# The input projection of a hybrid attention and mLSTM step as products of scaled float16 pairs

## The chip, the cores and the metric

The kernel runs on one core of one Trainium2 chip. The metric is the time of one execution on the device in microseconds; the median of three runs stands for a kernel. A core has five engines with instruction streams of their own: TensorE (PE, its weight loads shown apart as PEld), VectorE (DVE), ScalarE (ACT), GpSimd (POOL) and SyncE (SP), which here starts nearly all the DMA transfers. Each engine takes its instructions in order.

## What is computed

One layer of a diffusion backbone is applied to 128 context tokens and 1024 latent tokens with a model width of 1024. All weights and activations are float32. The part that matters here is the input projection `h @ w_in` and what reads it:

```python
def trunk_layer(x, mods, norm1_w, w_in, ...):
    sh1, sc1, g1, sh2, sc2, g2 = mods
    h = rmsnorm(x, norm1_w) * (1 + sc1) + sh1
    aq, ak, av, mq, mk, mv, mo, mg = jnp.split(h @ w_in, SPLIT_POINTS, axis=-1)
    aq = rmsnorm(aq, q_norm_w)
    ak = rmsnorm(ak, k_norm_w)
    ...
    attn_o = attention(aq, keys, vals)
    gates = mg + gate_bias
    hm = mlstm_bidir(heads(mq), heads(mk) * (MLSTM_DK ** -0.5), heads(mv), gates, ...)
    hm = rmsnorm(hm, mlstm_norm_w) * sigmoid(mo)
    x = x + g1 * (concat([attn_o, hm]) @ w_out)
    h2 = rmsnorm(x, norm2_w) * (1 + sc2) + sh2
    return x + g2 * swiglu(h2, w_gu, w_down), ...
```

The modulation (`sh1`, `sc1` and so on) is `silu(cond) @ w_ada + b_ada`. `w_in` has 1024 rows and 2832 columns: 512 for the attention queries, 128 for keys, 128 for values, four times 512 for the four mLSTM heads (query, key, value, output gate, 128 columns of each to a head) and 16 for the gates.

## The kernel before

**Pairs.** TensorE multiplies in a reduced float32 form (`F32R`). To keep accuracy, each operand is split into a high part that the form holds exactly and a low part, the rest; a product is the sum of three: high by high, high by low and low by high. `load_piece` (L139) does this for weights. A DMA brings two blocks of 128 rows into `raw` (two buffers), ScalarE casts it to `whi` (L152), and the difference goes to `wlo` (L135, called from L154) on POOL, with every third one on VectorE; there are five buffers of each.

**Tokens.** The 1152 tokens are nine blocks of 128: block 0 is the context, 1 to 8 the latents. Three blocks make a chunk of 384 columns. The normalised and modulated `h` is kept transposed, as pairs of tiles `hTh` and `hTl` for each chunk (L291 and L292), in six buffers `b0` to `b5`; later tiles of the attention use these buffers again.

**Stages, in the order in which they are written.** First the rows of `w_ada` for the first two modulations are multiplied (L248) and turned into columns (L254), which `modulation` adds and scales into `scale1` and `shift1` (L240, L243). Then comes the stage of `h`, with the keys, values and gates: the loads of the four key/value pieces (L307 to L315, tiles `kraw`, the rows of x for blocks 1 and 2 between them), and for each block the norm (L257 to L264), the transposes on PE (L114), the modulation into `full` (three of eight columns blocks on ScalarE, L332, the others on VectorE, L335), the high half (L341 on ScalarE, L343 on VectorE) and the low half on POOL (L344). `linear_tok` (L389) multiplies blocks of tokens with pieces of weights (L399 to L401; the tokens are the stationary side, the weights stream), two blocks at a time, and hands the sums to an evacuation: `evac_kvg` copies keys and values (L408, L409) and adds the bias to the gates (L410).

Then the four mLSTM heads follow. `head_project` (L643) loads the head's four pieces of 2 by 512 columns (`head_pieces`), multiplies the queries transposed, chunk by chunk (`q_group`, L670 to L672, 384 columns), and then keys, values and output gates block by block (`linear_tok`, 384 columns), with the evacuation L649 to L663. The scan of head h (`head_mlstm`, L683) is woven between the products of head h+1. Head 3's scan stands beside the first part of the attention queries (`QFIRST`, 512 columns); the rest of the queries follow. After that come the attention, the output projection and the feed-forward part, in which `w_gu` and `w_down` are multiplied (L1189 to L1191, L1008 to L1010); the attention's probabilities are multiplied with the values there as float16 pairs already (L942, L943).

**What sets the order.** `weave` and `emit` write the generators' steps one between the other. A planner then simulates the program and orders each engine's instructions; `hot(n)` raises the priority of what is emitted under it. The pools reuse buffers by tag: a new tile of a tag waits for the last reader of the one whose buffer it takes.

Of the kernel before, what the change touches and what calls it, by code (L numbers as in the profile page):

```python
# [8 lines left out]
F32 = mybir.dt.float32  # L9
# [36 lines left out]
def hybrid_step(ctx: ExitStack, tc: tile.TileContext, I: dict, O: dict):  # L46
# [24 lines left out]
    def emit(gen):  # L71
        for _ in gen:
            pass
# [45 lines left out]
    def rsqrt(tp, ss, n, inv, cap=24, plus=EPS):  # L119
# [38 lines left out]


# [22 lines left out]
    selb = gp.tile([P, 36], BF16, name="selb")  # L182

# [107 lines left out]
    hTh = [hp.tile([P, KD, CT], F32R, name=f"hTh{c}", tag=f"b{2 * c}") for c in range(NCH)]  # L291
    hTl = [hp.tile([P, KD, CT], F32R, name=f"hTl{c}", tag=f"b{2 * c + 1}") for c in range(NCH)]  # L292
# [14 lines left out]
    kvg = []  # L307
    for j in range(4):
        rows = w_in[2 * j * P : (2 * j + 2) * P, :].rearrange("(a p) n -> p a n", p=P)
        kvg.append(load_piece([  # L310
            (lambda v: v[:, :, 0:256], rows[:, :, 512:768]),
            (lambda v: v[:, :, 256:272], rows[:, :, 2816:2832]),
        ], (2, 272), 2, p0.tile([P, 544], F32, name=f"kraw{j}")))
        if j % 2:
            dma(xs[j // 2 + 1], xrow(j // 2 + 1))  # L315

    for b in range(CB, NB):
        dma(xs[b], xrow(b))
    for c in range(NCH):
        if c > 0:  # L320
            normalise(c * CB, CB)
        for i in range(CB):
# [4 lines left out]
            for half, ps in enumerate(xT[b] if b < 1 else transposed(b)):  # L327
# [16 lines left out]
                sub(hTl[c][:, half * 4 : half * 4 + 4, i * P : (i + 1) * P], full, hi.bitcast(F32), "pool")  # L344
# [61 lines left out]
    def evac_kvg(b, ps):  # L406
        bi = 9 if b == 0 else b - 1
        nc.scalar.copy(kall[:, bi], ps[:, 0:128].rearrange("p (h d) -> p h d", d=HD))  # L408
        nc.scalar.copy(vall[:, bi], ps[:, 128:256].rearrange("p (h d) -> p h d", d=HD))  # L409
        dve.tensor_tensor(  # L410
            out=Gv[:, :, :, 4 * b : 4 * b + 4],
            in0=ps[:, 256:272].rearrange("p (d t h) -> p d t h", d=2, t=2),
            in1=gbias.rearrange("p (d t h) -> p d t h", d=2, t=2), op=ALU.add)

    emit(linear_tok(kvg, 0, 272, evac_kvg))


# [123 lines left out]
    def square_pieces(src):  # L541
        return [load_piece([(full_view, src[2 * j * P : (2 * j + 2) * P, :].rearrange("(a p) n -> p a n", p=P))], (2, 512))
                for j in range(4)]

    def norm_rope(qp, cc, ss, x, nb, nh, w, rb):
# [6 lines left out]
        ssum = qp.tile([P, 20], F32, name=nm("nrs"), tag="nrs", bufs=2)[:, :n]  # L552
# [22 lines left out]
    def k_work(qp, cc, ss, kw):  # L575
# [7 lines left out]
        qone = qp.tile([1, P], F32, name="qone")  # L583
        dve.memset(qone, 1.0)
# [16 lines left out]
        mm(ps[:, 0:2], qone, v1[:, 2:4], start=True, stop=True)  # L601
# [3 lines left out]
    def evac_q(qp, cc, ss, qw):  # L605
        held = {}

        def evac(b, ps):
# [4 lines left out]
            nc.scalar.copy(qr[:, b - grp[0]], ps.rearrange("p (h d) -> p h d", d=HD))  # L613
# [20 lines left out]
    def head_pieces(h):  # L634
        pieces = []
        for j in range(4):
            rows = w_in[2 * j * P : (2 * j + 2) * P, 768:2816].rearrange("(a p) (t g n) -> p a t g n", p=P, t=4, g=NH)
            pieces.append(load_piece(
                [((lambda v, a=a: v[:, a, :].rearrange("p (t n) -> p t n", t=4)), rows[:, a, :, h, :]) for a in range(2)],
                (2, 512)))  # L640
        return pieces

    def head_project(h, st):  # L643

        pieces = head_pieces(h)
# [3 lines left out]
        def evac(b, ps):  # L649
            kt = mlp.tile([P, P], F32, name=nm("kt"), tag="kt", bufs=MB)  # L650
            act(kt, ps[:, 0:P], AF.Copy, scale=P ** -0.5)
            va = mlp.tile([P, P + 1], F32, name=nm("va"), tag="va", bufs=MB)
            dve.tensor_copy(va[:, 0:P], ps[:, P : 2 * P])
            pool.memset(va[:, P : P + 1], 1.0)
            th = mlp.tile([P, P], F32, name=nm("th"), tag="th", bufs=2)
            act(th, ps[:, 2 * P : 3 * P], AF.Tanh, scale=0.5)
# [8 lines left out]
        def q_group(cs):  # L665
# [8 lines left out]
            for ps, c in zip(banks, cs):  # L674
                qT = mlp.tile([P, CT], F32, name=nm("qT"), tag="qTm", bufs=2 * NCH)
                dve.tensor_copy(qT, ps[:, 0:CT])
                st["q"][c] = qT
# [744 lines left out]
```

## Time and profile before

| | us |
|---|---|
| median of three runs (smallest, largest) | 1618.56 (1618.33, 1621.84) |
| the profiled execution | 1619.03 |
| its span, first to last instruction | 1617.1 |

The stages lie like this in the profiled execution:

| stage | us from the start of the span |
|---|---|
| products with `w_ada` for the first two modulations | 7 to 27 |
| `h`, keys, values, gates | 28 to 82 |
| mLSTM heads 0, 1, 2, 3, with the scan of the head before | 82 to 393 |
| attention queries | 393 to 466 |
| attention and output projection | 456 to 640 |
| feed-forward, with the rest of the attention | 622 to 1617 |

The profile's pages are read as follows. "Busy" is the time in which an engine had an instruction under way; matmuls overlap, so that the busy time of one is longer than the distance to the next. A group of instructions is named by its line in the code, engine and operation, by the tiles it writes and reads (`out<-in`), by its shape and its count; behind the bar stand the busy time and the mean length of one in ns, then the idle time before them with what ended it. In a timeline the first number is the start and the second the length. A table of windows gives, for each stretch of the span, the busy microseconds of each engine with its count of instructions, the mean clock granted to TensorE (1.00 is full), the busy share of the DMA engines and what they moved.

### The profile page before, as it was taken

Reading aid. Unit: us, or ns where it says so; the run is one execution under the profiler, and the core shown is the slowest. Engines: PE = TensorE matmul, PEld = TensorE weight load, DVE = VectorE, ACT = ScalarE, POOL = GpSimd, SP = SyncE. Lnnn points to the kernel's source line nnn. Section 1 sums busy time; section 2 is a strip of 40 time slices with the busy share of each in tenths; the row PEclk is TensorE's granted clock in tenths of the full one; section 3 lists DMA queues with packets and bytes.
Section 4 is the critical chain, followed back from the end, with each engine's and each line's share of the span. In section 5 each row is a group of like instructions: output and inputs, shape, how many; then the busy total and the mean of one; then the engine's idle time right before and its main releaser. Section 6 shows DMA issues by size and latency. Waiting matters only on the chain. (4 is left out here: it accounts for less than half of the span.)

```text
span 1617.1 us, 23358 instructions
## 1 busy us (share of the span) xinstructions
PE 1532.5 (95%) x8670; PEld 1366.1 (84%) x8670; DVE 965.3 (60%) x1969; ACT 689.8 (43%) x1193; POOL 618.0 (38%) x392
## 2 busy tenths in 40 slices
PE   6899999899898968999999999999999999999996
PEld 2888888898676757998989899898898989999995
DVE  4842363957877668577663646767674474432445
ACT  3522242424534556555643344565552453333322
POOL 1511030413345324443445344444344445544443
PEclk8999999999898988999999999999999999999998
DMA  9244443303155865777773446777684445534441
GB/s 358 67 155 125 117 142 52 82 22 71 50 183 134 180 153 116 174 181 178 180 179 113 148 153 216 188 179 175 156 185 131 131 144 176 151 127 146 144 130 65
DMA packets 386311, 232.71 MB, mean 144 GB/s; under 512 B 169910, under 2 KB 346502, under 8 KB 386198
## 3 DMA queue, kind: packets, MB, share of 16 engines
q1 hardware_dynamic: 384342, 228.04, 52.5%
q10 hardware_dynamic: 1856, 3.19, 0.6%
q8 instruction: 68, 1.11, 0.3%
q14 instruction: 45, 0.37, 0.1%
HBM read 181.16 MB, written 11.69 MB: 119 GB/s over the span
## 5 line engine op out<-in xcount | busy, mean ns | idle before, releaser
L135 POOL TENSOR_TENSOR wlo<-raw,whi 128x1024 fp32r<-128x1024 f32 (+1 forms) x159 | 390.2, 2459 | 512.3 <-ACT whi L152 474.4
L152 ACT CAST whi<-raw 128x1024 fp32r<-128x1024 f32 x239 | 245.0, 1026 | 361.7 <-DMA raw<-in_w_gu_dram 112.8
L1190 PE MATMUL mm<-aTl,whi 128*128 128x384 f32 (+2 forms) x1088 | 363.6, 334 | 0.0
L1189 PE MATMUL mm<-aTh,whi 128*128 128x384 f32 (+2 forms) x1088 | 362.5, 335 | 0.8 <-DVE tn L1217 0.8
L1191 PE MATMUL mm<-aTh,wlo 128*128 128x384 f32 (+2 forms) x1088 | 363.2, 334 | 0.0
L1189 PEld LDWEIGHTS mm<-aTh,whi 128*128 128x128 f32 x1088 | 204.5, 188 | 2.2 <-DVE tn L1217 1.4
L1190 PEld LDWEIGHTS mm<-aTl,whi 128*128 128x128 f32 x1088 | 204.9, 188 | 0.7
L1191 PEld LDWEIGHTS mm<-aTh,wlo 128*128 128x128 f32 x1088 | 204.9, 188 | 0.2
L135 DVE TENSOR_TENSOR wlo<-raw,whi 128x1024 fp32r<-128x1024 f32 (+1 forms) x80 | 98.4, 1230 | 151.7 <-ACT whi L152 147.8
L1008 PE MATMUL mm<-whi,hl 128*128 128x512 f32 x372 | 146.4, 398 | 0.8 <-ACT hl L1221 0.7
L1009 PE MATMUL mm<-wlo,hl 128*128 128x512 f32 x372 | 146.9, 396 | 0.0
L1010 PE MATMUL mm<-whi,hl 128*128 128x512 f32 x372 | 144.3, 396 | 0.8 <-POOL hl L135 0.8
L399 PE MATMUL wi<-whi,hTh 128*128 128x384 f32 (+2 forms) x392 | 135.9, 347 | 5.2 <-ACT hTh L341 5.1
L925 DVE SCALAR_TENSOR_TENSOR pl<-pr,st,ph 128x1152 f16<-128x1152 f32 (+1 forms) x72 | 111.6, 1550 | 47.7 <-ACT ph L924 47.6
L401 PE MATMUL wi<-whi,hTl 128*128 128x384 f32 (+2 forms) x392 | 133.6, 343 | 1.3 <-POOL hTl L135 1.3
L400 PE MATMUL wi<-wlo,hTh 128*128 128x384 f32 (+2 forms) x392 | 133.5, 341 | 0.0
L921 ACT ACTIVATE pr<-S,st 128x1152 f32<-128x1152 f32 (+1 forms) x72 | 81.2, 1128 | 99.7 <-DVE st L920 90.6
L135 POOL TENSOR_TENSOR hl<-tn,hl 128x384 fp32r<-128x384 f32 x66 | 83.5, 1266 | 105.0 <-ACT hl L1221 104.9
L998 DVE TENSOR_TENSOR x<-x,t 128x512 f32<-128x512 f32 x102 | 116.9, 1168 | 0.8
L1217 DVE SCALAR_TENSOR_TENSOR tn<-tn,mm 128x384 f32<-128x384 f32 (+2 forms) x68 | 36.6, 539 | 134.2 <-PE mm L1191 100.4
L918 PE MATMUL S<-kst,qT 128*128 128x384 f32 (+1 forms) x400 | 88.1, 356 | 13.9 <-ACT pr L921 13.8
L920 DVE TENSOR_REDUCE st<-S 128x1 f32<-128x1152 f32 (+1 forms) x72 | 88.8, 1233 | 20.7 <-PE S L918 20.3
(323 smaller groups left out, 2714.2 us busy)
## 6 DMA issues: line engine op xcount, KB each, us to landing
raw<-in_w_gu_dram SPq DMA_DIRECT2D x132, 512.0 KB, 4.0
raw<-in_w_down_dram SPq DMA_DIRECT2D x60, 512.0 KB, 3.6
a<-in_w_ada_dram SPq DMA_DIRECT2D x32, 512.0 KB, 4.2
gl<-g_d SPq DMA_DIRECT2D x36, 256.0 KB, 3.8
aw<-in_w_ada_dram SPq DMA_DIRECT2D x16, 512.0 KB, 8.9
raw<-in_w_in_dram SPq DMA_DIRECT2D x32, 256.0 KB, 5.6
raw<-in_w_out_dram SPq DMA_DIRECT2D x15, 512.0 KB, 4.9
x<-in_x_sample_dram SPq DMA_DIRECT2D x13, 512.0 KB, 6.4
```

Of the source, the lines that this page charges most:

```text
L135: (dve if eng == "dve" else pool).tensor_tensor(out=out, in0=full, in1=hi, op=ALU.subtract)
L152: nc.scalar.copy(hi[:, :n], raw[:, :n])
L399: mm(ps[:, :n], ah, wh[:, k % 2, c0 : c0 + n], start=(k == 0), stop=False)
L400: mm(ps[:, :n], ah, wl[:, k % 2, c0 : c0 + n], start=False, stop=False)
L401: mm(ps[:, :n], al, wh[:, k % 2, c0 : c0 + n], start=False, stop=(k == KD - 1))
L998: eng.tensor_tensor(out=x1[:, cs], in0=x1[:, cs], in1=t, op=ALU.add)
L1008: mm(ps, ah, wh[:, k % 2, :], start=(k == 0), stop=False)
L1009: mm(ps, ah, wl[:, k % 2, :], start=False, stop=False)
L1010: mm(ps, al, wh[:, k % 2, :], start=False, stop=(k == nk - 1))
L1189: mm(ps, wh[:, k, :], th[:, k, :], start=(k == 0), stop=False)
L1190: mm(ps, wh[:, k, :], tl[:, k, :], start=False, stop=False)
L1191: mm(ps, wl[:, k, :], th[:, k, :], start=False, stop=(k == KD - 1))
```

## The change

The products with `w_in` use pairs of float16 in place of pairs of reduced float32. Since float16 has a narrow range, both sides are scaled by powers of two first, and the evacuations take the scale out again.

- For `h`, the scale comes from a bound on the modulation: the greatest of `scale1` times the root of the width, plus the greatest of `shift1`. `powers` turns a bound into a power of two and its inverse with bit operations, and `scale1` and `shift1` are multiplied before the first `full`.
- For the weights, each group (key/value/gates, four heads, queries) gets one scale. `Scaled.ready` loads the four raw tiles, sums the absolute values of their rows on ScalarE, takes the maximum on VectorE and brings it to one number with `power_scale`: a transpose on PE, a maximum over the row, `powers`, and a product with a row of ones (`one1`) that spreads the two numbers over the partitions.
- `Scaled.pairs` makes the halves. Of every second piece, ScalarE makes the high half with the scale in the cast and VectorE the low half in one fused operation; of the others, ScalarE scales the raw tile in place and copies it, and POOL subtracts. For the key/value group all four go the first way.
- `hT` holds both halves in one float16 tile for each chunk, in buffers `b3` to `b5`.
- The key/value loads stand ahead of all the rows of x; the raw tiles of a head's weights are loaded and summed while the head before is multiplied; those of head 0 and the sums go beside the key/value products.
- Evacuations use scales from tiles. The gates' evacuation is two operations for each block instead of one. Two small buffers of `rsqrt` and the norm shrink from 24 and 20 columns to 16.

The number of products and their shapes stay: 1152 of 384 columns, 216 of 512 and 216 of 272. Each float16 matmul has its weight load as an instruction of its own.

```diff
+    def powers(v, n):
+        v = v[0:n]
+        dve.tensor_scalar(out=v[:, 0:1], in0=v[:, 0:1], scalar1=2.0 ** -16, scalar2=None, op0=ALU.max)
+        dve.tensor_scalar(out=v[:, 1:2].bitcast(I32), in0=v[:, 0:1].bitcast(I32), scalar1=0x7F800000, scalar2=None, op0=ALU.bitwise_and)
+        dve.tensor_scalar(out=v[:, 2:3].bitcast(I32), in0=v[:, 1:2].bitcast(I32), scalar1=-1, scalar2=266 * 2 ** 23, op0=ALU.mult, op1=ALU.add)
+        dve.tensor_scalar(out=v[:, 3:4], in0=v[:, 1:2], scalar1=2.0 ** -12, scalar2=None, op0=ALU.mult)
+
+    def power_scale(tp, one, bound, out):
+        ps = bank()
+        transpose(ps[0:1, 0:P], bound)
+        v = tp.tile([1, 4], F32, name=nm("pv"), tag="pv", bufs=2)
+        dve.tensor_reduce(out=v[:, 0:1], in_=ps[0:1, 0:P], axis=AX.X, op=ALU.max)
+        powers(v, 1)
+        yield
+        ps = bank()
+        mm(ps[:, 0:2], one, v[:, 2:4], start=True, stop=True)
+        dve.tensor_copy(out, ps[:, 0:2])
+        yield
+
+    class Scaled:
...
+        def ready(self):
+            a, b = self.shape
+            n = self.n = a * b
+            raws = self.raws or [wp.tile([P, 1024], F32, name=nm("iraw"), tag="wlo", bufs=5) for _ in self.srcs]
...
+                    dma(part(raw[:, :n].rearrange("p (a b) -> p a b", b=b)), ap_)
+            yield
+            t = gp.tile([P, 12], F32, name=nm("isc"), tag="isc", bufs=3)
+            for j, raw in enumerate(raws):
+                jk = wp.tile([P, 1024], BF16, name=nm("jk"), tag="raw", bufs=2)
+                act(jk[:, :n], raw[:, :n], AF.Abs, accum_out=t[:, j : j + 1])
+                yield
+            dve.tensor_reduce(out=t[:, 4:5], in_=t[:, 0:4], axis=AX.X, op=ALU.max)
+            dve.tensor_tensor(out=t[:, 4:5], in0=t[:, 4:5], in1=hsc[:, 3:4], op=ALU.mult)
+            yield from power_scale(gp, one1, t[:, 4:5], t[:, 6:8])
+            dve.tensor_tensor(out=t[:, 8:9], in0=t[:, 6:7], in1=hsc[:, 3:4], op=ALU.mult)
+            dve.tensor_scalar(out=t[:, 9:10], in0=t[:, 7:8], scalar1=P ** -0.5, scalar2=None, op0=ALU.mult)
+            dve.tensor_scalar(out=t[:, 10:11], in0=t[:, 7:8], scalar1=0.5, scalar2=None, op0=ALU.mult)
+            self.scale, self.inv, self.inv_k, self.inv_half = t[:, 8:9], t[:, 7:8], t[:, 9:10], t[:, 10:11]
+
+        def pairs(self, dve_every=2):
...
+                w = wp.tile([P, 2, 1024], F16, name=nm("ipair"), tag="whi", bufs=5)
+                hi, lo = w[:, 0, :n], w[:, 1, :n]
+                if j % dve_every == dve_every - 1:
+                    act(hi, raw[:, :n], AF.Copy, scale=self.scale)
+                    dve.scalar_tensor_tensor(out=lo, in0=raw[:, :n], scalar=self.scale, in1=hi, op0=ALU.mult, op1=ALU.subtract)
+                else:
+                    act(raw[:, :n], raw[:, :n], AF.Copy, scale=self.scale)
+                    nc.scalar.copy(hi, raw[:, :n])
+                    sub(lo, raw[:, :n], hi, "pool")
...
-    hTh = [hp.tile([P, KD, CT], F32R, name=f"hTh{c}", tag=f"b{2 * c}") for c in range(NCH)]
-    hTl = [hp.tile([P, KD, CT], F32R, name=f"hTl{c}", tag=f"b{2 * c + 1}") for c in range(NCH)]
+    hT = [hp.tile([P, 2, KD, CT], F16, name=f"hT{c}", tag=f"b{3 + c}") for c in range(NCH)]
+    hTh, hTl = [t[:, 0] for t in hT], [t[:, 1] for t in hT]
+
+    dve.tensor_reduce(out=hs2, in_=shift1, axis=AX.XY, op=ALU.max, apply_absolute_value=True)
+    dve.tensor_reduce(out=hsc[:, 0:1], in_=scale1, axis=AX.XY, op=ALU.max, apply_absolute_value=True)
+    dve.scalar_tensor_tensor(out=hsc[:, 0:1], in0=hsc[:, 0:1], scalar=float(D) ** 0.5, in1=hs2, op0=ALU.mult, op1=ALU.add)
+    powers(hsc, P)
+    for t in (scale1, shift1):
+        dve.tensor_scalar(out=t, in0=t, scalar1=hsc[:, 2:3], scalar2=None, op0=ALU.mult)
...
+    kvg_steps = kvg.ready()
+    next(kvg_steps)
+    for b in range(1, CB):
+        dma(xs[b], xrow(b))
     for b in range(CB, NB):
         dma(xs[b], xrow(b))
...
+    steps = groups_in[0].ready()
+    next(steps)
...
+            if b == 0:
+                with hot(300):
+                    emit(kvg_steps)
+                    kvg_pairs = kvg.pairs(1)
...
-        nc.scalar.copy(kall[:, bi], ps[:, 0:128].rearrange("p (h d) -> p h d", d=HD))
+        act(kall[:, bi], ps[:, 0:128].rearrange("p (h d) -> p h d", d=HD), AF.Copy, scale=kvg.inv)
...
-    emit(linear_tok(kvg, 0, 272, evac_kvg))
+    weave(linear_tok(kvg_pairs, 0, 272, evac_kvg), steps, 40, 8)
+    emit(steps)
...
     def head_project(h, st):
-        pieces = head_pieces(h)
+        w = groups_in[h]
+        pieces = w.pairs()
+        nxt_steps = groups_in[h + 1].ready()
+        next(nxt_steps)
...
-            act(kt, ps[:, 0:P], AF.Copy, scale=P ** -0.5)
+            act(kt, ps[:, 0:P], AF.Copy, scale=w.inv_k)
-            dve.tensor_copy(va[:, 0:P], ps[:, P : 2 * P])
+            dve.tensor_scalar(out=va[:, 0:P], in0=ps[:, P : 2 * P], scalar1=w.inv, scalar2=None, op0=ALU.mult)
...
-        yield from linear_tok(pieces, P, 3 * P, evac)
+        for i, _ in enumerate(linear_tok(pieces, P, 3 * P, evac)):
+            if i % 4 == 3:
+                next(nxt_steps, None)
+            yield
+        emit(nxt_steps)
```

More of the change, by code (lines that the diff above doesn't have):

```diff
@@ L182, in hybrid_step @@
     selb = gp.tile([P, 36], BF16, name="selb")
+    one1 = gp.tile([1, P], F32, name="one1")
+    hsc = gp.tile([P, 4], F32, name="hsc")
+    hs2 = gp.tile([P, 1], F32, name="hs2")
+    dve.memset(one1, 1.0)
     es0 = ExitStack()
@@ L600, in k_work @@
         ps = bank()
-        mm(ps[:, 0:2], qone, v1[:, 2:4], start=True, stop=True)
+        mm(ps[:, 0:2], one1, v1[:, 2:4], start=True, stop=True)
         dve.tensor_copy(vsc[:, 0:2], ps[:, 0:2])
```

66 lines of the change are left out of this document (32 added, 34 removed).

## The prediction

> **What bounds the kernel now.** I read the page first, then a table of windows of 10 us, then single engines' timelines at the seams it showed.
>
> ```profile
> span 1617.1 us, 23358 instructions
> PE 1532.5 (95%) x8670; PEld 1366.1 (84%) x8670; DVE 965.3 (60%) x1969; ACT 689.8 (43%) x1193; POOL 618.0 (38%) x392
> ```
>
> The profiled execution took 1619.03 us, so 1.9 us lie around its span, and it stands 0.5 us above the median of 1618.56. TensorE is nearly always busy, but an average of 95% says nothing of a stage. The windows do (columns: PE, PEld, DVE, ACT, POOL, granted clock, DMA share, GB/s):
>
> ```profile
> 30.00:40.00 10.00, 4.61 (x18) 3.97 (x18) 8.96 (x34) 8.75 (x17) 4.32 (x3) 0.55 1.01 377
> 50.00:60.00 10.00, 8.38 (x59) 7.72 (x57) 9.79 (x23) 2.75 (x7) 5.83 (x4) 0.92 0.35 96
> 70.00:80.00 10.00, 10.00 (x83) 10.00 (x81) 7.16 (x20) 5.76 (x13) 6.76 (x7) 1.00 0.10 31
> 300.00:310.00 10.00, 8.05 (x52) 7.27 (x50) 9.93 (x31) 5.63 (x13) 4.86 (x6) 1.00 0.37 107
> 420.00:430.00 10.00, 7.18 (x52) 5.96 (x52) 9.88 (x49) 7.57 (x29) 3.02 (x6) 1.00 0.08 29
> ```
>
> Three regimes follow. From 30 to about 70 us the h and key/value stage hangs on VectorE (9.79 of 10). From 70 us through three heads PE is full at clock 1.00: there a shorter matmul is worth its full length. Around 290 to 330 and 390 to 430 us VectorE is full again (9.93, 9.88) and PE has holes: there a shorter matmul is worth nothing and an added VectorE operation costs its length. Behind 640 us PE is full with products that the change doesn't touch, so a delay or gain ahead of them arrives at the end undiminished.
>
> **The narrower products.** A busy matmul row overlaps the next, so I take the distance from start to start (columns: start, us, then the instruction). The first pair of rows lies 15 matmuls of 384 columns apart, the second 15 of 512, the third 27 fp32r of 256, the last 8 float16 of 256:
>
> ```profile
> 100.48 0.33 PE L399 MATMUL wi<-whi,hTh 128*128 128x384 f32 x1
> 103.08 0.34 PE L399 MATMUL wi<-whi,hTh 128*128 128x384 f32 x1
> 445.14 0.39 PE L400 MATMUL mm<-wlo,hTh 128*128 128x512 f32 x1
> 448.64 0.40 PE L400 MATMUL mm<-wlo,hTh 128*128 128x512 f32 x1
> 630.27 0.28 PE L1189 MATMUL mm<-aTh,whi 128*128 128x256 f32 x1
> 633.46 0.28 PE L1189 MATMUL mm<-aTh,whi 128*128 128x256 f32 x1
> 1169.81 0.27 PE L942 MATMUL po<-phT,vs 128*128 128x256 f16 x1
> 1170.69 0.27 PE L942 MATMUL po<-phT,vs 128*128 128x256 f16 x1
> ```
>
> That is 2.60/15 = 173 ns, 3.50/15 = 233 ns, 3.19/27 = 118 ns and 0.88/8 = 110 ns. So float16 gains 8 ns on 118. The trace has no float16 matmul of 384 or 512 columns. If the gain is a fixed 8 ns, 384 columns come to 165 ns; if it goes with width (0.932 times), to 161 ns and 217 ns. I take a saving of 10.5 ns at 384 and 14.5 ns at 512, between both ends (8 to 12, 8 to 16), nearer the proportional one because the fp32r rows themselves lie on a line of 0.45 ns a column. The Trainium skill ("TensorE: Matmul & The Clock Gate", section "Back-to-back issue gap") gives N/2.4 + 2.5 ns for a warm isolated matmul, 109 ns at 256, which the 110 ns agree with; by it 384 and 512 columns would take an estimated 162.5 and 216 ns.
>
> How many there are (columns: count, then busy us and mean ns):
>
> ```profile
> L399 PE MATMUL wi<-whi,hTh 128*128 128x384 f32 x288 | 100.6, 349 | 0.0
> L670 PE MATMUL wi<-hTh,whi 128*128 128x384 f32 x96 | 33.8, 353 | 0.0
> L399 PE MATMUL mm<-whi,hTh 128*128 128x512 f32 x40 | 17.3, 433 | 4.0 <-DVE nu L758 2.5 <-ACT qraw L613 1.5
> L399 PE MATMUL wi<-whi,hTh 128*128 128x512 f32 x32 | 12.7, 398 | 0.0
> ```
>
> Each line is one of three products, so the four heads have 3 x (288 + 96) = 1152 matmuls and the queries 3 x 72 = 216. A head saves 288 x 10.5 ns = 3.0 us. Heads 0 and 1 run wholly in full-PE time; of the 6.0 us of heads 2 and 3 I count 4.6, since each meets a stretch in which VectorE rules. Heads: **-10.6 us**. Of the queries only the 3 x 40 of the second pass run with PE as the bound: **-1.7 us**. The 216 key/value matmuls of 272 columns shorten inside the VectorE-bound stage: 0. With nothing but this, 1619.0 would become 1606.7.
>
> **The start of the h stage.** Now the first modulated `full` on VectorE stands early:
>
> ```profile
> 30.61 0.41 DVE L335 TENSOR_SCALAR full<-mm,scale,shift 128x128 f32<-128x128 f32 x1
> 31.21 0.15 DVE L126 TENSOR_SCALAR rh<-rv 128x1 int32<-128x1 int32 x1
> 31.39 0.15 DVE L127 TENSOR_SCALAR ry<-rh 128x1 int32<-128x1 int32 x1
> 32.06 0.64 ACT L152 CAST whi<-kraw 128x544 fp32r<-128x544 f32 x1 [0.55 <-DMA kraw<-in_w_in_dram]
> 32.97 0.63 ACT L152 CAST whi<-kraw 128x544 fp32r<-128x544 f32 x1
> ```
>
> In the changed order VectorE reaches `full` only behind the maximum over the four absolute row sums of the key/value pieces and then ten small dependent operations (the maxima of scale1 and shift1, the power of two, two multiplications). The fourth piece is in by 32.97 now; it moves ahead of x1 in SyncE's queue, so I let its Abs end near 32.6. Small dependent operations start 0.18 to 0.19 us apart (31.21, 31.39). That gives 32.6 + 10 x 0.19 = 34.5 for the first `full`: +3.9 us. Lower end +2, if the pieces land as much sooner as two x loads of 512 KB take; upper end +6, if the sums wait behind x's Square on ScalarE. Queued behind are the transposes' evacuations, the float16 halves, and PE's key/value products.
>
> To the end of the stage VectorE gets: four fused lo halves (L217) in place of two subtractions, some 20 small operations of two scale chains, and two operations per G evacuation where there was one.
>
> ```profile
> 75.16 1.20 DVE L343 CAST hTh<-full 128x512 fp32r<-128x512 f32 x1 [0.53 <-ACT full L332]
> 76.44 1.29 POOL L135 TENSOR_TENSOR hTl<-full,hTh 128x512 fp32r<-128x512 f32 x1 [0.36 <-DVE G L410]
> 34.06 0.71 DVE L135 TENSOR_TENSOR wlo<-kraw,whi 128x544 fp32r<-128x544 f32 x1
> L410 DVE TENSOR_TENSOR G<-wi,gbias 128x16 f32<-128x16 f32 x9 | 1.4, 164 | 0.0
> ```
>
> Two more halves at 0.71 are 1.4 us, nine small operations for the stage's own chain and seven for head 0's 16 x 0.17 = 2.7, nine more G operations 1.5: 5.6 in all. VectorE has 0.2 to 1.3 us of air per 10 us here, and POOL loses two subtractions that ran beside it, so I count +3. The last lo half on POOL then lies near 84.6.
>
> Head 0 follows. ScalarE used to make a hi half with one cast; now it makes, in this order, a scaled copy in place of pieces 0 and 2 and then the hi half of piece 0, and POOL's lo half follows.
>
> ```profile
> L152 ACT CAST whi<-raw 128x1024 fp32r<-128x1024 f32 x227 | 237.6, 1048 | 334.0 <-DMA raw<-in_w_gu_dram 112.8 <-PE mm L1190 56.1 <-DMA raw<-in_w_down_dram 49.3
> L135 POOL TENSOR_TENSOR wlo<-raw,whi 128x1024 fp32r<-128x1024 f32 x153 | 382.6, 2504 | 500.6 <-ACT whi L152 462.7 <-issue 14.7 <-DVE t L997 12.9
> L135 DVE TENSOR_TENSOR wlo<-raw,whi 128x1024 fp32r<-128x1024 f32 x74 | 94.3, 1274 | 127.1 <-ACT whi L152 123.3 <-DMA a<-in_w_ada_dram 3.5
> 81.83 0.34 PE L670 MATMUL wi<-hTh,whi 128*128 128x384 f32 x1
> ```
>
> 3 x 1.05 + 2.50 = 5.6 us against 1.05 + 1.27 = 2.3 now, 3.3 us more, about half of it under the last key/value products: +1.7. So the first product of head 0 moves from 81.8 to about 90.4. Start in all: **+8.6 us**, ends +5 and +11.
>
> **The heads.** Each group costs ScalarE four Abs with a sum, which the Square of x prices, and two more passes; and evacuations take their scale from a tile instead of a constant.
>
> ```profile
> L261 ACT ACTIVATE jk<-x 128x1024 bf16<-128x1024 f32 x9 | 9.5, 1056 | 1.4 <-DMA x<-in_x_sample_dram 0.9 <-DMA x<-in_x_prompt_dram 0.2
> L261 ACT ACTIVATION_READ_ACCUMULATOR jk<-x 128x1 f32 x9 | 1.7, 190 | 0.0
> L651 ACT ACTIVATE kt<-wi 128x128 f32<-128x128 f32 x36 | 9.4, 277 | 74.9 <-PE wi L401 74.9
> L751 ACT ACTIVATE it<-mm,QT 128x129 f32<-128x129 f32 x64 | 20.1, 369 | 7.4 <-PE mm L748 5.7 <-DVE nu L758 1.2 <-DVE dn L765 0.3
> L653 DVE COPY va<-wi 128x128 f32<-128x128 f32 x36 | 10.1, 283 | 16.9 <-ACT kt L651 13.9 <-PE mm L755 2.8
> L335 DVE TENSOR_SCALAR full<-mm,scale,shift 128x128 f32<-128x128 f32 x45 | 16.2, 402 | 1.9 <-ACT full L332 1.6
> L925 DVE SCALAR_TENSOR_TENSOR pl<-pr,st,ph 128x1152 f16<-128x1152 f32 x64 | 105.3, 1645 | 47.1 <-ACT ph L924 47.0
> ```
>
> ScalarE: 4 x (1.06 + 0.19) + 2 x 1.05 = +7.1 us a group, and 18 evacuations at up to 369 in place of 277, +1.7. It was 43% busy and the raws of the next head are loaded, summed and scaled during the current one, so PE's own work hides it; without that cover it would be 9 us a head. VectorE: eleven small operations (1.9), two fused halves at 1.32 (1645 x 1024/1152, 1.46, at most) for 1.33 subtractions at 1.27 (+1.2), nine va copies at up to 402 for 283 (+1.1): +4.2 a group, free where PE is full. In the two stretches of VectorE it is not: the part that falls there (one chain, nine evacuations, one of the two halves, and the query group's) I put at +1.8 and +1.5, **+3.3 us** (ends 0 and +6). The four products with `one1` and the transposes before them sit in PE's order and wait for VectorE's small operations; a late one holds up every matmul behind it. I count half a microsecond for each of four or five, **+2.2** (ends 0 and +8). POOL has 2 instead of 2.67 subtractions a group: nothing, as it isn't the bound.
>
> From 456 us on only buffers change (three tiles of h leave), and the order of PE's products stays: 0, ends -4 and +4.
>
> **Sum:** 1619.0 - 10.6 - 1.7 + 8.6 + 3.3 + 2.2 = 1620.8; I say **1621 us**.
>
> **Rivals.**
> *A, the delays hide.* If the raws' earlier loads and the spare time on POOL let the stage end only 4 us late, and VectorE's additions find the holes, the toll is 4 + 1 and the time 1619.0 - 12.3 + 5 = 1612. For it: PE was full already at 70 us, ahead of the last h halves. Against: VectorE at 9.79, in order.
> *B, the scaled pairs come late at every head.* The pair tiles have five buffers for four pieces, so a head's first pairs wait for the last products of the head before; then the copy, the float16 half and POOL's 2.5 us run with PE idle. If each of four boundaries shows 3 us of hole more, that is 12 us: 1633. It decides once ScalarE reaches the next pieces less than 3.6 us (1.05 + 2.50) before PE has run out. For it: ScalarE's 9 us more a head, and its evacuations in the same queue. Against: PE shows no hole at any boundary of the first three heads now.
> *C, float16 at 384 columns is no faster than fp32r,* because each product now carries a weight load as an instruction of its own, of this length (columns: count, busy us, mean ns):
>
> ```profile
> L942 PEld LDWEIGHTS <-vs 128*128 128x128 f16 x292 | 29.1, 100 | 26.0 <-issue 9.5 <-DVE oT L947 6.1 <-DMA phT<-ph 5.9
> ```
>
> Then the 12.3 us are gone: 1633. Against: the 110 ns rows carry such loads too.
> *D, float16 products of 384 columns overlap until only the 100 ns of the weight load part them.* That saves 73 ns on each of 1152, and from 1633 the heads alone lead to 1549. Against: at 256 columns they stand 110 ns apart, not 100, and a row of 233 ns at 512 shows no such overlap. The same section of the Trainium skill states a sustained 131 ns per matmul at 512 columns for pairs of load and matmul, which would go this way; no row here bears it out.
>
> **How the numbers follow.** Forecast 0.45, its own range 1614 to 1628; A 0.26; B 0.18; C 0.09; D 0.02. Within 0.2%, 3.2 us, is what a measurement can't tell from no change (1615.3 to 1621.8). Of the forecast's own case I put 0.04 below, 0.19 within and 0.22 above; A gives 0.25 faster and 0.01 within, B and C are slower, D faster: 0.31, 0.20, 0.49. The range runs from 1608 (A with proportional savings and a start of +3) to 1635 (B with the upper end of the stretches); about 0.15 is left out.
>
> **What would show it.** First `full` near 34.5 us, first product of head 0 near 90, start distances of 161 to 165 ns at 384 and about 218 at 512, PE full to about 290, and the two VectorE stretches longer by 1 to 2 us each. A start under 86 speaks for A; holes of 3 us at head boundaries for B; 173 ns for C. The prediction is wrong if the attention stage from 456 us moves by more than 4 us either way, since I gave it nothing.

## The result and the profile after

| | before | after |
|---|---|---|
| median, us (smallest to largest of 5 runs) | 1618.56 (1618.16 to 1623.24) | 1627.82 (1622.25 to 1632.99) |
| span of the profiled execution, us | 1617.1 | 1626.0 |

The ratio is 1.0046, with a 95% interval of 1.0028 to 1.0065: slower by half a per cent. It lies inside the range, 0.2 us below the end of the forecast's own (1614 to 1628), and on the side that had the greatest chance, but by another sum than the one that was forecast. Measured again beside three other kernels, the same kernel came to 1622.43 us, 1.0010 times the kernel before (1.0000 to 1.0020). So the loss is 0.1 to 0.5%, and the executions of the changed kernel seem to scatter more: over 10.7 us in 5 runs and 8.5 in 11, where those of the kernel before kept within 5.1 in 5 and within 6.8 to 8.9 in three rounds of 23.

The head of the page and the table of windows of the changed kernel (window, then PE, PEld, DVE, ACT, POOL, granted clock, DMA share, GB/s):

```profile
span 1626.0 us, 23528 instructions
PE 1517.4 (93%) x8688; PEld 1258.8 (77%) x8688; DVE 970.8 (60%) x2059; ACT 732.5 (45%) x1251; POOL 606.5 (37%) x387
```

```profile
30.00:40.00 10.00, 1.33 (x4) 0.68 (x4) 7.56 (x47) 8.75 (x19) 2.27 (x2) 0.58 1.01 385
50.00:60.00 10.00, 7.81 (x58) 5.82 (x58) 9.69 (x30) 6.61 (x15) 3.46 (x3) 0.95 0.17 48
70.00:80.00 10.00, 10.00 (x88) 8.45 (x86) 8.22 (x33) 6.45 (x16) 6.72 (x8) 1.00 0.09 24
300.00:310.00 10.00, 4.15 (x17) 2.28 (x18) 9.61 (x18) 7.36 (x16) 4.83 (x3) 0.73 0.33 84
```

TensorE is busy 15 us less in a span that is 9 us longer. The window from 30 us shows the late start, that from 70 us that the start was made up, and that from 300 us holds the seam before head 3, which lay later and was spread wider before; the part on the prediction compares the whole of it.

Following a few instructions of TensorE through both traces shows where the time went. The table gives their starts in us. The last query product stands for the last of the high-by-high ones; two more follow within half a microsecond. The 112th score product is the last of the first attention chunk, and behind the 161st TensorE is nearly full to the end (the recorded expectations count that one as the 160th):

| | before | after | difference |
|---|---|---|---|
| first key/value product | 34.2 | 39.4 | +5.2 |
| first product of head 0 | 81.8 | 82.4 | +0.6 |
| first token product of head 3 | 327.7 | 321.2 | -6.5 |
| last query product | 465.4 | 455.7 | -9.7 |
| 112th score product | 601.1 | 599.4 | -1.7 |
| 161st score product | 700.3 | 705.9 | +5.6 |
| end of the span | 1617.1 | 1626.0 | +8.9 |

The change does what it was meant to up to the last query product, 9.7 us ahead. Then the attention stage gives back 15.3 us, and the feed-forward part another 3.3. These 3.3 us are within the scatter: in the fourteen profiles here that part takes 916.8 to 921.1 us, the least in the kernel before. The windows from the last query product to the 161st score product, the first of the kernel before, the second of the changed one, in fences of their own:

```profile
465.00:700.00 235.00, 203.63 (x1122) 171.53 (x1120) 169.78 (x300) 124.75 (x185) 97.43 (x54) 0.92 0.69 163
```

```profile
456.00:706.00 250.00, 207.53 (x1125) 173.61 (x1124) 164.24 (x306) 126.27 (x189) 97.65 (x55) 0.90 0.63 148
```

The number of products is about the same (1122 and 1125). Of the 15 us more, TensorE idles 11.1 (42.5 against 31.4), and for the rest it is "busy" at a lower clock. What it waits for there, grouped by waiter and releaser (us in total, times, longest), in the kernel before and then in the changed one:

```profile
PE S L918 <- ACT pr L921: 12.2, 7, 2.9
PE po L942 <- DMA phT<-ph: 4.9, 2, 4.5
PE po L942 <- DVE oT L947: 4.8, 2, 4.3
```

```profile
PE S L1000 <- ACT pr L1003: 17.7, 8, 3.7
PE po L1025 <- DMA plT<-pl: 6.2, 5, 2.2
PE po L1024 <- DMA phT<-ph: 5.9, 3, 5.2
PE po L1024 <- ACT pr L1003: 4.5, 1, 4.5
```

These are links of the softmax chain: scores wait until ScalarE has taken the exponentials of the last ones, the values wait for the transposed probabilities. The change touches none of these instructions. The experiments ask why they cost more.

### The profile page after: what moved, and what is told of

Read it like the earlier page. It is cut to its first block, busy times and chain, and to the rows that moved or that the text cites. A ratio compares the mean times of both kernels' runs of the same rounds, so it can differ in the third digit from the quotient of the medians.

```text
span 1626.0 us, 23528 instructions
## 1 busy us (share of the span) xinstructions
PE 1517.4 (93%) x8688; PEld 1258.8 (77%) x8688; DVE 970.8 (60%) x2059; ACT 732.5 (45%) x1251; POOL 606.5 (37%) x387
## 5 line engine op out<-in xcount | busy, mean ns | idle before, releaser
L135 POOL TENSOR_TENSOR wlo<-raw,whi 128x1024 fp32r<-128x1024 f32 x146 | 357.8, 2454 | 445.7 <-ACT whi L152 407.9
L152 ACT CAST whi<-raw 128x1024 fp32r<-128x1024 f32 x219 | 224.4, 1025 | 375.9 <-DMA raw<-in_w_gu_dram 137.8
L135 DVE TENSOR_TENSOR wlo<-raw,whi 128x1024 fp32r<-128x1024 f32 (+1 forms) x73 | 88.1, 1206 | 142.2 <-ACT whi L152 141.7
L1007 DVE SCALAR_TENSOR_TENSOR pl<-pr,st,ph 128x1152 f16<-128x1152 f32 (+1 forms) x72 | 107.8, 1498 | 39.4 <-ACT ph L1006 39.4
L488 PE MATMUL wi<-ipair,hT 128*128 128x384 f16 (+2 forms) x392 | 128.2, 327 | 2.8 <-ACT ipair L216 2.8
L489 PE MATMUL wi<-ipair,hT 128*128 128x384 f16 (+2 forms) x392 | 128.1, 327 | 0.0
L490 PE MATMUL wi<-ipair,hT 128*128 128x384 f16 (+2 forms) x392 | 127.1, 326 | 0.0
L135 POOL TENSOR_TENSOR hl<-tn,hl 128x384 fp32r<-128x384 f32 x66 | 84.2, 1276 | 105.0 <-ACT hl L1303 105.0
```

The lines of the kernel that those rows point to most:

```text
L135: (dve if eng == "dve" else pool).tensor_tensor(out=out, in0=full, in1=hi, op=ALU.subtract)
L152: nc.scalar.copy(hi[:, :n], raw[:, :n])
L488: mm(ps[:, :n], ah, wh[:, k % 2, c0 : c0 + n], start=(k == 0), stop=False)
L489: mm(ps[:, :n], ah, wl[:, k % 2, c0 : c0 + n], start=False, stop=False)
L490: mm(ps[:, :n], al, wh[:, k % 2, c0 : c0 + n], start=False, stop=(k == KD - 1))
```

## The experiments

For each kernel below, the table gives the start of the last query product, the length from there to the 161st score product ("stage"), and the span, all from its profile, with the median and the ratio of its runs to the kernel before on the same chip.

| kernel | last query product | stage | span | median | ratio (95%) |
|---|---|---|---|---|---|
| before | 465.4 | 234.9 | 1617.1 | 1618.56 | 1 |
| changed | 455.7 | 250.2 | 1626.0 | 1627.82 | 1.0046 (1.0028 to 1.0065) |
| a_again, the same | 452.9 | 246.3 | 1617.3 | 1622.43 | 1.0010 (1.0000 to 1.0020) |
| a_const | 445.8 | 253.5 | 1620.4 | 1621.34 | 1.0004 (0.9991 to 1.0017) |
| a_tags | 457.6 | 245.0 | 1622.8 | 1620.20 | 1.0000 (0.9987 to 1.0013) |
| a_tags_const | 446.7 | 247.7 | 1613.8 | 1614.69 | 0.9969 (0.9955 to 0.9983) |
| a_nq | 449.8 | 254.7 | 1622.4 | 1624.81 | 1.0036 (1.0023 to 1.0048) |
| b_minus | 450.7 | 236.1 | 1606.5 | 1610.56 | 0.9944 (0.9926 to 0.9961) |
| b_plus | 474.1 | 237.6 | 1632.6 | 1635.80 | 1.0102 (1.0084 to 1.0120) |
| a_w10 | 451.3 | 247.8 | 1616.8 | 1620.30 | 1.0003 (0.9990 to 1.0016) |
| a_w12 | 458.1 | 229.5 | 1605.7 | 1611.11 | 0.9945 (0.9930 to 0.9959) |
| a_w12_nq | 463.9 | 230.7 | 1613.1 | 1612.13 | 0.9954 (0.9942 to 0.9965) |
| b_w10 | 461.8 | 249.5 | 1630.4 | 1632.25 | 1.0075 (1.0063 to 1.0088) |
| b_w12 | 473.3 | 237.2 | 1631.0 | 1631.31 | 1.0067 (1.0051 to 1.0083) |

**Is a gain ahead of the attention stage lost in it?** The first theory was that the stage, paced by its softmax chain, takes what comes sooner. The kernel before, with 12.5 us of TensorE time taken out of head 0 or put in:

```diff
-                    mm(ps[:, :n], al, wh[:, k % 2, c0 : c0 + n], start=False, stop=(k == KD - 1))
+                    for x in range(lows):
+                        mm(ps[:, :n], al, wh[:, k % 2, c0 : c0 + n], start=False, stop=(x == lows - 1 and k == KD - 1))
...
-        yield from linear_tok(pieces, P, 3 * P, evac)
+        yield from linear_tok(pieces, P, 3 * P, evac, lows=0 if h == 0 else 1)
```

In the second kernel `lows` is 2 for head 0.

> The kernel before, without the low-by-high product of head 0's keys, values and output gates: 72 matmuls of 173 ns less, 12.5 us of TensorE time in a stretch where TensorE is full. Leaves out that part of the product. Theory 1 (the attention stage takes what is gained ahead of it): the last query product comes about 12 us sooner than 465.8 us, and the time falls by less than 6 us from 1618.6. Theory 4 (the stage passes a gain on, and the changed kernel lost it for a reason of its own): 1606.

> The kernel before with the same 72 products done twice: 12.5 us more TensorE time in head 0. The second sum enters the result. Theory 1: the last query product comes 12 us later, and the attention stage makes up part of it, so that the time rises by less than 8 us. Theory 4: 1631.

The time fell by 9.3 us and rose by 16.0, on either side of the 12.5 of the fourth theory; the spans moved by -10.6 and +15.5. The last query product moved by -14.7 and +8.7 us, and the stage was 236.1 and 237.6 us against 234.9. So the first theory fell: the stage as such passes a gain or a delay on, nearly whole. TensorE's order in it is partly another in these two kernels, but from the last output products on it is the old one, and its length hardly changed: not every new order is a slow one.

**What do the scales cost?** The changed kernel with constants:

```diff
-            t = gp.tile([P, 12], F32, name=nm("isc"), tag="isc", bufs=3)
...
-            self.scale, self.inv, self.inv_k, self.inv_half = t[:, 8:9], t[:, 7:8], t[:, 9:10], t[:, 10:11]
+            self.scale, self.inv, self.inv_k, self.inv_half = 256.0, 2.0 ** -14, 2.0 ** -14 * P ** -0.5, 2.0 ** -15
...
-        dve.tensor_scalar(out=t, in0=t, scalar1=hsc[:, 2:3], scalar2=None, op0=ALU.mult)
+        dve.tensor_scalar(out=t, in0=t, scalar1=64.0, scalar2=None, op0=ALU.mult)
```

> The changed kernel with the three scales as constants (64 for h, 256 for w_in, 2^-14 back): no absolute sums, no maxima, no power products, constants in the evacuations. Theory 1 (the scales cost little, the loss is made in the attention stage): the first product of head 0 about 1 to 4 us sooner than the 82.4 us of the changed kernel, the last query product about 2 to 5 us sooner than 456 us, and the time still not below the kernel before by more than those few us: 1618 to 1628. Theory 2 (the scale chains and the dearer evacuations are what eats the saving): the time falls to about 1608 to 1612.

The first product of head 0 came at 81.8 us, 0.6 us sooner, where 1 to 4 were expected. The last query product came at 445.8 us, 7 to 10 us before that of the changed kernel's two profiles (452.9 and 455.7), where 2 to 5 were expected. The time, 1621.3 us, was inside the first theory's range: the stage, at 253.5 us, had taken the gain, though its work is the same. TensorE's order differs from the first key/value products (38.6 us) on here, so that the 7 to 10 us hold the price of the scales with whatever the new order brought.

**Do the freed buffers matter?**

```diff
-    hT = [hp.tile([P, 2, KD, CT], F16, name=f"hT{c}", tag=f"b{3 + c}") for c in range(NCH)]
+    hT = [hp.tile([P, 2, KD, CT], F16, name=f"hT{c}", tag=f"b{c}") for c in range(NCH)]
```

> The changed kernel with the three tiles of h in buffers b0 to b2 instead of b3 to b5; nothing else. Theory 1 (what counts is how the softmax chain is fed, not which buffers are free): the key stacks and the first scores wait for the last query products as in the kernel before, the output projection's inputs come free sooner, and the time moves by less than 4 us from 1627.8. Theory 3 (the moved buffers let the mLSTM half of the output projection run ahead and so leave TensorE without work later): the holes between 560 and 620 us shrink by 10 us and the time falls to about 1617.

The time was 1620.2 us: 7.6 below the changed kernel's first median, 2.2 below the second. TensorE's idle time between 560 and 620 us fell to 17.1 us, from 26.0 in the first profile of the changed kernel and 22.0 in the second. That is near the 10 us of the third theory against the first profile alone; the stage became only 5.2 and 1.3 us shorter, and against the repeat the time moved too little for this theory. TensorE's order is that of the changed kernel up to the last query products and another one behind them, so that what the free buffers do and what the new order does can't be told apart here. With both edits:

> The changed kernel with both constant scales and the tiles of h in b0 to b2. If what each of the two gained alone comes from different stretches, the two add up: last query product at 446 to 448 us, 137 us from there to the last score of the first attention chunk, and a time of about 1612 to 1614. If the length of the attention stage depends on the order that the planner happens to find, it is not the sum: anything from 1605 to 1622.

1614.7 us, 0.3% less than the kernel before and just above the 1612 to 1614 of the sum. The last query product came at 446.7 us as added up, the 112th score product 136.1 us behind it as expected; then 111.6 us passed to the 161st, where the two edits alone had 105.5 and 107.9. The numbers fit both readings.

**A hole behind a load.** In the first profile of the changed kernel TensorE stood still for 4.4 us in the middle of head 1, for a piece of `w_ada`:

```profile
167.50 0.64 PE L318 MATMUL mm<-a,silp 128*32 128x256 f32 x8 [4.43 <-DMA a<-in_w_ada_dram]
```

Two small writes of scan states stand before these loads in SyncE's queue. The next kernel moves them to ScalarE's queue (`nc.scalar.dma_start` for the writes of `new_state_C` and `new_state_n`); TensorE's order is unchanged.

> The changed kernel with the eight small writes of new_state_C and new_state_n of the scans on ScalarE's DMA queue instead of SyncE's; TensorE's order is as in the changed kernel. Theory 5 (behind these writes the queue's loads crawl from 154 to 166 us, and the faster products of head 1 bring TensorE to a w_ada piece that is still on its way): the hole of 4.4 us at 163 us and the half clock behind it vanish, the first product of head 1's token part comes at 162 to 163 us instead of 168, and the time falls by about 5 us from the changed kernel's. Rival (the loads crawl for another reason than the queue): hole and time stay.

The hole shrank to 1.33 us, which looked like the theory; the time, 1624.8 us, fell by 3.0 of the expected 5, but lies above the 1622.4 us of the repeat. The repeat of the changed kernel, with nothing moved, has this row at the same place:

```profile
165.94 0.64 PE L318 MATMUL mm<-a,silp 128*32 128x256 f32 x8 [1.78 <-DMA a<-in_w_ada_dram]
```

So most of the hole was the luck of one execution. Without the moved writes it is 1.62, 1.76 and 2.08 us in three other kernels with the same order up to there (a_tags, a_w12, a_w10). The same edit on the fastest kernel:

> The fastest kernel so far (weave at 24 to 12) with the writes of the scan states on ScalarE's DMA queue; TensorE's order is that of the kernel without this. Theory 5 (the small writes hold up the loads behind them on one queue): 2 to 4 us less than the 1611.1 us. Rival: no difference beyond 1.5 us.

1612.1 us beside 1611.1 without it, each as a ratio inside the other's interval, and its hole was 3.23 us against 1.76. The small writes ahead of the loads are not the cause; why the loads crawl there stays open.

**The planner's order.** What was left is the order itself. `weave` places the attention steps between the last query products, 11 steps to 24. One number, in each kernel, to 10 or 12:

```diff
-    weave(linear_tok(w_q, 0, 512, ev_q, QREST, bank), chain(key_stacks(), att), 24, 11)
+    weave(linear_tok(w_q, 0, 512, ev_q, QREST, bank), chain(key_stacks(), att), 24, 12)
```

The work is the same, and so is TensorE's order up to 419 to 440 us, in the second pass of the query products.

> The changed kernel with one number of the planner's input moved: the weave of the last query products with the first attention steps at 24 to 12 instead of 24 to 11. No work is added or taken away. Theory 6 (the stage from the last query product to the full-TensorE time hangs on the planner's order, in which this change stirred as any other would): the stage's length moves by 5 us or more in either direction, while all that lies ahead of 440 us stays where it is. Rival (the stage's length is set by the softmax chain): it moves by less than 3 us.

> The same number moved in the kernel before. Theory 6: its stage (135.7 us from the last query product to the last score of the first chunk, 99 us from there to the 160th score product) becomes longer by 5 us or more, if the order that it had was a lucky one. Rival: within 3 us of 1618.6.

> The changed kernel with the weave at 24 to 10. Theory 6 (planner's order): all ahead of 440 us as in the changed kernel; TensorE's order behind it has the tail of the kernels with the constant scales and with the moved tiles (all eight transposes, then the scores, then a block of 47 feed-forward products), which took 105 to 108 us from the last score of chunk 0 to the 160th against 99.2 in the kernel before. So that stretch again takes 105 to 108 us; the time lies anywhere from 1612 to 1632. Rival (the stage's length belongs to the float16 change): within 3 us of 1627.8.

> The kernel before with the weave at 24 to 10: here the planner finds the same tail as in the changed kernels, without any float16 product in the input projection. Theory 6: the stretch from the last score of chunk 0 to the 160th takes 104 us or more instead of 99.2, and the time rises by 5 us or more. Rival (the tail is slow because of something in the change): that stretch stays at 99 to 101 us.

> The changed kernel once more, beside the others on one chip. Expected 1624 to 1629. The hole behind the loads of w_ada at 163 us, 4.4 us in the first profile, shows whether it is a fixture of the order (3 us or more again) or the luck of one execution (under 2 us).

The changed kernel with 12 took 1611.1 us, 0.55% less than the kernel before; the kernel before with 12 and with 10 took 1631.3 and 1632.3, 0.67 and 0.75% more. The changed kernel with 10 took 1620.3 us: that misses the rival's 1627.8, but it lies within 3 us of the repeat, which itself came below its expected 1624 to 1629. With the numbers 11, 12 and 10 the stage of the float32 kernel is 234.9, 237.2 and 249.5 us long, that of the float16 kernel 246.3 to 254.7 (three profiles of one order, with a_nq), 229.5 and 247.8.

The start of the stage moves with the number as well, since it decides how many attention steps stand between the last query products. In the kernel before with 12 the last query product came 7.9 us later and the stage grew by only 2.3 us, less than the 5 that the sixth theory expected. The first query product lies ahead of every difference in order. From it to the 161st score product the float32 kernel takes 318.7, 328.2 and 330.0 us with 11, 12 and 10; the float16 kernel takes 328.6 to 335.7, 318.4 (324.9 with the writes moved) and 328.0. Counted so, each kernel has one order that is shorter than its other two, by up to 17 us, while profiles of one order differ by up to 7. These are the windows of the stage in the changed kernel with 12 and then in the kernel before with 10:

```profile
458.00:688.00 230.00, 200.40 (x1121) 168.33 (x1119) 167.66 (x297) 123.43 (x183) 97.78 (x55) 0.94 0.70 158
```

```profile
462.00:711.00 249.00, 209.28 (x1119) 175.99 (x1119) 170.77 (x301) 125.44 (x186) 95.71 (x55) 0.90 0.64 154
```

The same 1119 to 1121 products leave TensorE 29.6 us idle at a mean clock of 0.94 in the one, 39.7 us at 0.90 in the other. Their first waits, in the same order:

```profile
PE S L1000 <- ACT pr L1003: 14.0, 9, 4.8
PE po L1024 <- DMA phT<-ph: 6.0, 2, 4.5
```

```profile
PE S L918 <- ACT pr L921: 18.4, 8, 4.6
PE po L942 <- DMA phT<-ph: 7.5, 5, 4.2
PE po L943 <- DMA plT<-pl: 4.9, 5, 1.3
```

A long stage without any float16 in the projection has the same signature as that of the changed kernel (17.7, 5.9 and 6.2 us), and a short one exists with it. That the order alone can move the time by as much as was lost is shown. That the changed kernel's 11 to 15 us are all of this kind is the reading that fits, but it isn't shown, since no kernel has float16 products and the old order. Another expectation missed: the tail that I took for the mark of a slow order (105 to 108 us from the 112th to the 161st score product) passed in 100.2 us in the float16 kernel with 10, and took 111.7 us in the float32 kernel with 10. Which link of the order costs the time is open.

**What the change itself is worth.** Over the three weaves the ratios of the float32 kernels are 1, 1.0067 and 1.0075, with a mean of 1.0047; those of the float16 kernels 1.0010 (1.0046 in the first measurement), 0.9945 and 1.0003, with a mean of 0.9986 (0.9998). The difference is 0.5 to 0.6%, 8 to 10 us in favour of the change, near the 9.7 and 12.5 us that it is ahead at the last query product. At the first query product, which the weave number doesn't touch, the seven profiles of float16 kernels with computed scales stand at 368.8 to 373.7 us, those of the float32 kernels with 10, 11 and 12 at 381.3 to 382.3: a lead of 7.6 to 13.5 us. Three orders each are few, and they differ among themselves by more than the two means do, so that the 0.5 to 0.6% is a hint and no measurement; but the kernel before stood on the best of its three.

## Why the prediction was right or wrong

The forecast was 1621 us by a start 8.6 us late, products 12.3 us shorter, tolls of 5.5 us and an attention stage that doesn't change. Measured were 1627.8 us, and 1622.4 in the repeat, beside which the kernel before took 1620.2.

**The narrower products: right.** Start distances in the changed kernel, 21 matmuls of 384 columns apart, then 6 of 512:

```profile
107.09 0.33 PE L489 MATMUL wi<-ipair,hT 128*128 128x384 f16 x1
110.50 0.33 PE L489 MATMUL wi<-ipair,hT 128*128 128x384 f16 x1
438.02 0.38 PE L490 MATMUL mm<-ipair,hT 128*128 128x512 f16 x1
439.31 0.38 PE L490 MATMUL mm<-ipair,hT 128*128 128x512 f16 x1
```

3.41/21 = 162 ns and 1.29/6 = 215 ns, a saving of 11 and 18 ns where 10.5 and 14.5 were taken. The 18 lies above the upper end of 16, worth half a microsecond on the 120 products counted. That excludes rivals C and D. The formula that the Trainium skill gives ("TensorE: Matmul & The Clock Gate", section "Back-to-back issue gap") would have an estimated 162.5 and 215.8 ns, and the trace agrees; its sustained 131 ns at 512 columns is not what this stream of loads and matmuls does.

**The start: the chain was right, what follows from it wrong.** Rows of VectorE, ScalarE and POOL in the changed kernel:

```profile
32.25 0.16 DVE L201 TENSOR_REDUCE isc<-isc 128x1 f32<-128x4 f32 x1 [2.60 <-ACT jk L199]
33.90 0.41 DVE L420 TENSOR_SCALAR full<-mm,scale,shift 128x128 f32<-128x128 f32 x1
75.78 0.87 DVE L428 CAST hT<-full 128x512 f16<-128x512 f32 x1
76.73 1.16 POOL L135 TENSOR_TENSOR hT<-full,hT 128x512 f16<-128x512 f32 x1 [0.36 <-DVE hT L428]
82.38 0.33 PE L747 MATMUL wi<-hT,ipair 128*128 128x384 f16 x1
84.17 0.50 PE L749 MATMUL wi<-hT,ipair 128*128 128x384 f16 x2 [0.98 <-POOL ipair L135]
```

VectorE waits 2.6 us for the sums and reaches the first `full` at 33.9 us; 34.5 was predicted. But the last high half comes at 75.8 us, 0.6 us later than before, where the sum put it 7 us later, and the first head product at 82.4 instead of 90.4. The step that failed is "to the end of the stage I count +3": from the first `full` to the last cast 44.55 us passed before (30.61 to 75.16) and 41.88 after, 2.7 us less. It was priced as a sum of added VectorE operations, 5.6 us, and the relief that the working named was credited with only 2.6 of them. The time was made up before 62 us: the eighth of the 18 low halves on POOL starts at 61.34 us before and 61.53 after, and from there to the last one both kernels take the same, 15.1 and 15.2 us. Ahead of that VectorE lost less time in small operations. One of the norm (L127) and the POOL rows beside it, in the kernel before:

```profile
50.28 1.78 DVE L127 TENSOR_SCALAR ry<-rh 128x3 int32<-128x3 int32 x1
49.66 2.38 POOL L135 TENSOR_TENSOR wlo<-raw,whi 128x1024 fp32r<-128x1024 f32 x1
51.98 1.29 POOL L135 TENSOR_TENSOR hTl<-full,hTh 128x512 fp32r<-128x512 f32 x1
```

and in the same operation of the changed kernel, where no POOL subtraction runs:

```profile
45.65 0.16 DVE L127 TENSOR_SCALAR ry<-rh 128x3 int32<-128x3 int32 x1
```

The long one ends with POOL's subtraction. Of the 48 small operations of the norm between 28 and 62 us, eight are stretched so before, to 0.73 to 1.78 us, and five after, to 0.71 to 1.15; all 48 take 15.6 us before and 11.5 after. The changed kernel has three subtractions of weights fewer on POOL there (28.58, 32.78 and 49.66 us before). The 4.0 us are half of the 8.3 that lie between the 5.6 added and the 2.7 gained; no run isolates this cause, and the other half stays open. Rival A was right on the start. The scaled pairs of head 0 cost TensorE only the wait of 0.98 us at 84.2, since the planner puts the products that need the low halves of the weights last: from the last high half to the first product of head 0 6.6 us pass, 6.7 before, where the sum had 1.7 more.

**The heads: most prices right.** kt with the scale from a tile, two passes and the sums, in the changed kernel:

```profile
L728 ACT ACTIVATE kt<-wi,isc 128x128 f32<-128x128 f32 x36 | 12.6, 366 | 67.6 <-PE wi L490 63.0 <-PE mm L786 3.9
L199 ACT ACTIVATE jk<-iraw 128x1024 bf16<-128x1024 f32 x20 | 21.2, 1058 | 7.6 <-DMA iraw<-in_w_in_dram 7.3 <-issue 0.3
L219 ACT ACTIVATE iraw<-iraw,isc 128x1024 f32<-128x1024 f32 x10 | 10.9, 1140 | 2.1 <-DVE isc L204 2.1
L730 DVE TENSOR_SCALAR va<-wi,isc 128x128 f32<-128x128 f32 x36 | 12.4, 346 | 16.9 <-ACT kt L728 12.7 <-PE mm L836 3.4 <-ACT it L832 0.4
L217 DVE SCALAR_TENSOR_TENSOR ipair<-iraw,isc,ipair 128x1024 f16<-128x1024 f32 x10 | 16.0, 1612 | 8.6 <-ACT ipair L216 8.6
```

366 and 1058 ns were foreseen (369, 1056); va was bounded at 402 and took 346; the fused half took 1.61 us where 1.46 was called the most. From the first head product to the last query product TensorE needed 383.6 us before and 373.3 after, 10.3 less. The sum had 12.3 less 5.5, 6.8; the products alone would give 1152 x 11 + 216 x 18 ns = 16.6 if all had counted. Tolls were there, among them the hole at 163 us, a queue that I hadn't looked at, and the seam before head 3. Here is that seam, before and then after:

```profile
280.00:340.00 60.00, 53.88 (x331) 49.91 (x330) 48.07 (x164) 18.35 (x63) 22.33 (x29) 1.00 0.27 70
```

```profile
280.00:340.00 60.00, 53.78 (x344) 36.43 (x342) 47.49 (x166) 23.62 (x65) 20.39 (x27) 0.94 0.29 78
```

TensorE is idle as long as before, but the clock is lower. Its idle time now stands in three holes of 1.32, 1.85 and 2.85 us between 300 and 308 us that wait for the scaled pairs from ScalarE, POOL and VectorE. Those are rival B's holes, at this one seam and not at every head.

**The attention stage: wrong.** "From 456 us on only buffers change, and the order of PE's products stays: 0, ends -4 and +4" is the step on which the total hangs, and it was off by 11 to 15 us. The order of PE's products did not stay: behind the start of the stage the two kernels' orders agree without a break only from about 840 us on. The prediction named a move of this stage by more than 4 us as what would make it wrong. That the total came near 1621 is luck, errors against each other: in the first profile 8.0 us too much at the start and 3.5 in the heads and queries, against 15.3 too little here and 3.3 behind it.

## What to carry to other kernels

Where a planner orders a stage that has waits in it, an edit anywhere before it draws a new order, worth as much as the edit: here 12 us for one weave number in the float32 kernel and 9 to 17 in the float16 one. Judge such a change up to the last point whose order is untouched, then try a few neutral orders of both kernels before you drop it or keep it. And when operations are added to a busy engine, look at which of its present ones are stretched and by what: here fewer stretched operations went with a stage that came out shorter, although the sum of the additions was 5.6 us.

## What the runs showed of the hardware

TensorE ran at half rate for a while behind its holes. After holes of 5.25 and 2.01 us in the changed kernel these rows stand 11 matmuls apart, 214 ns each, where the same 256 columns took 110 ns in the kernel before at full clock, so that the 11 cost 1.1 us more:

```profile
573.45 0.42 PE L1024 MATMUL po<-phT,vs 128*128 128x256 f16 x1
575.80 0.42 PE L1025 MATMUL po<-plT,vs 128*128 128x256 f16 x1
```

The row is busy in the profile; only the granted clock, 0.66 between 560 and 580 us, tells it from good work. An operand from a tile instead of a constant costs ScalarE 89 ns on a 128x128 evacuation (366 against 277); the Trainium skill ("ScalarE: Activation LUTs", section "What ACT_TABLE_LOAD costs") gives about 93 ns for each such operand, and the trace agrees. A small VectorE operation that meets a GpSimd subtraction can last until this ends: the thirteen stretched ones of the h stage took 0.71 to 1.78 us and ended within 0.03 us of it, where 0.16 us is their length without one. And one order of instructions isn't one time: two profiles of the changed kernel lie 8.7 us apart (1626.0 and 1617.3), with its runs from 1616.9 to 1633.0 us.
